# A decoder trunk on one core: x loaded tile by tile into another ring, its squares taken off GpSimd, small loads queued later

## The chip, the cores and the metric

The kernel runs on one core of one Trainium2 chip. The metric is the time of one execution in microseconds (us), lower is better. Three runs of the kernel before took 2304.75, 2304.87 and 2307.06 us, median 2304.87 us. The core has a matrix engine (TensorE, "PE" in the profile, with its weight loads "PEld"), a vector engine (VectorE, "DVE"), an activation engine (ScalarE, "ACT"), a general engine (GpSimd, "POOL") and a queue engine (SyncE, "SP") that only issues DMA transfers. ACT and POOL issue DMA transfers too, each on a queue of its own.

## The reference

One decoder layer in float32, 512 tokens of width 2048. Three sub-layers follow one another, each on a root-mean-square norm of x and added back to x: a mixer of three head groups (dilated window attention A, forgetting attention B, gated linear attention C), a cross-attention into 256 memory tokens, and a gated feed-forward network with a short causal convolution. A last norm closes it. The part that the change touches is the very first step:

```
def rms_norm(x, g):
    y = x * rsqrt(mean(x * x, axis=-1) + EPS)
    return y * g

proj = rms_norm(x, norm_mix) @ w_in     # 2048 -> 6168, split into the three groups' inputs
```

## The kernel before, in words

**Number format.** Each float32 operand of a large product is split in two parts of a faster format, `hi` (a rounded copy, made on ACT) and `lo` (the rest, made on DVE), and each product is three matmuls: hi by hi, hi by lo, lo by hi. So a weight tile needs one ACT and one DVE instruction for each half (L355, L356 in `weights`), and a tile of x needs one of each too (L322, L323 in `split_to`; they fold in the norm's gain, from a small table `gains`).

**x and its layout.** x is held transposed: 16 tiles, each 128 features by 512 tokens (256 KB). In memory two tiles lie side by side, in 512 KB blocks.

**The first stage.** `mixer` begins with `nat_units` on `w_first` (408 columns: the values of three head pairs of group A, the forget gates and the rank-16 gate). It has eight units. Unit u loads one block of weights (408 KB; L344) and works on the x tiles 2u and 2u+1. Four accumulators in PSUM, one for each 128 tokens, stay open over all 16 tiles; a tile of x meets each in three matmuls (L410 to L412). That is 192 matmuls of 408 columns. `xtile(k)` is called when a unit first needs tile k: it loads, splits and squares it. For k even, `raw_tile` loads the pair of tiles in one transfer (L1034); the first pair alone goes in two (L1032).

**The rings.** The pairs of x lie in the same ring of five 4 KB slots (`wraw`, WR = 5) as the raw weight blocks, in turn: weights, pair, weights, pair. A load waits until the last reader of its slot is done. The split weights have a ring of five half blocks (WS = 5). A ring of six tiles, `str`, in the pool `mc` (`stream`), is not used until later: it then holds parts of the mixer's output and the first six tiles of the residual.

**The sums of squares.** `square` adds the squares of the tiles up in two tiles `ls` (even k and odd k). Tiles 0 and 1 are squared on POOL directly (L1040); for the others ACT makes the square (L1044) and DVE adds it for odd k, POOL for even k (L1046). After tile 15, `stats` takes the sums over features with 16 narrow matmuls (L436), and DVE and POOL make the factor of each token from it, `rsx` (L439, L440). The accumulators are read out with that factor (`evac_v` at L629 and L630, then L890).

**Small loads.** The identity (64 KB), the causal mask `tri` (64 KB) and the convolution's coefficients `conv` (86 KB) are loaded on ACT's queue; the identity at L248, the others written after the first stage (L893, L894) but free to go earlier. The small operands of the gates and of the relative bias are loaded on POOL's queue (L642 to L726), 12 transfers, each ordered behind `self.begun`, which is POOL's addition for x tile 6.

**What sets the order.** The program is written in Python order; a planner then puts the instructions of each engine into a fixed order by modelled times and priorities, and each engine runs its list strictly in that order, waiting where data are missing. `issue_after` adds one fixed order between two instructions of an engine. Eight warm-up matmuls on a tile of ones come first on PE (L253).

After the first stage come the other input projections, with the gates, the relative bias and the gated linear attention worked in between, then attention A and B, the output projection, cross-attention and the feed-forward network, which holds half of the time.

Of the kernel before, what the change touches and what calls it, by code (L numbers as in the profile page):

```python
# [12 lines left out]
F32 = mybir.dt.float32  # L13
F32R = mybir.dt.float32r
I32 = mybir.dt.int32
AF = mybir.ActivationFunctionType
ALU = mybir.AluOpType
AX = mybir.AxisListType

P = 128  # L20
D = 2048
KT = D // P
S = 512
# [19 lines left out]
HT = S // 2  # L43
# [30 lines left out]
W_X = 8  # L74
WARM = 8
M0 = 8
H0 = 4
H1 = 6
ST = 4
# [148 lines left out]
class _Trunk:  # L228
    def __init__(self, tc, es, d, out):
        self.tc, self.es, self.nc, self.d, self.out = tc, es, tc.nc, d, out  # L230
        nc = tc.nc
        self.con = es.enter_context(tc.tile_pool(name="con", bufs=1))
        self.wp = es.enter_context(tc.tile_pool(name="wp", bufs=1))
        self.mc = es.enter_context(tc.tile_pool(name="mc", bufs=1))
        self.ps = es.enter_context(tc.tile_pool(name="ps", bufs=1, space=bass.MemoryType.PSUM))
        self.dr = es.enter_context(tc.tile_pool(name="dr", bufs=1, space=bass.MemoryType.DRAM))
        edge = es.enter_context(tc.tile_pool(name="edge", bufs=1, side="right"))
        edge.tile([P, 8], F32, name="edge")
        self.es_xp = ExitStack()
        self.xp = self.pool(self.es_xp, "xp", "right")  # L240
        self.bg = deque()
        self.credit = self.rate = 0
        nc.scalar.preload_act_table_set("natural_log_exp_and_others")
        con = self.con
        self.gains = con.tile([P, 5 * KT], F32, name="gains")
        nc.scalar.dma_start(out=self.gains, in_=d["gains"])
        self.ident = con.tile([P, P], F32, name="ident")
        nc.scalar.dma_start(out=self.ident, in_=d["c_ident"])  # L248
        self.ones = con.tile([P, P], F32, name="ones")
        nc.gpsimd.memset(self.ones, 1.0)  # L250
        warm = self.pst("W")
        for _ in range(WARM):
            nc.tensor.matmul(warm[:, :P], self.ones, self.ones, start=True, stop=True)  # L253
        self.eps = con.tile([P, 1], F32, name="eps")
        nc.gpsimd.memset(self.eps, EPS)
        self.onesr = con.tile([P, P], F32R, name="onesr")
        nc.scalar.activation(self.onesr, self.ones, AF.Copy)
        self.mhalf = con.tile([P, 16], F32, name="mhalf")
        nc.gpsimd.memset(self.mhalf, -0.5)
        self.conv = con.tile([P, 4 * FT], F32, name="conv")  # L260
        self.tri = con.tile([P, P], F32, name="tri")

    def pool(self, es, name, side):
        return es.enter_context(self.tc.tile_pool(name=name, bufs=1, side=side, reuse_waits="tile"))
# [594 lines left out]
    def mixer(self):  # L859
        nc, d, tc = self.nc, self.d, self.tc  # L860
# [15 lines left out]
        xs = {}  # L876
        parts = [self.pretile([P, S], i) for i in range(2)]

        def xtile(k):
            if k not in xs:  # L880
                raw = self.raw_tile(d["xT"], k, S, k == 0)
                xs[k] = self.split_gain(raw, self.gain(0, k))
                self.square(k, raw, parts, lambda n: self.pretile([P, n], 2 + k % 2))
                if k == KT - 1:
                    self.rs, self.spread = self.stats(parts, S, "x")
            return xs[k]

        def evac_first(t, ps):
            self.evac_v(t, ps, "a", 0, 3)
            self.turn = nc.scalar.activation(self.fg[:, t, :], ps[:, 384:G0], AF.Copy, scale=self.rs[:, t:t + 1])  # L890

        self.run(self.nat_units(d["w_first"], 0, xtile, NT, evac_first, True))
        nc.scalar.dma_start(out=self.tri, in_=d["c_tri"])  # L893
        nc.scalar.dma_start(out=self.conv, in_=d["conv"])  # L894
        xl = [xs[k] for k in range(KT)]

        def evac_c(dst, scale, j):
# [88 lines left out]
        for n in range(4, KT):  # L986
            for u in units[n]:
                u()
                if n >= M0:
                    next(mem, None)  # L990
# [32 lines left out]
        if sqs is not None:  # L1023
            self.square(dt, x1, sqs, tmp)

    def raw_tile(self, src, k, n, split=False):
        per = 1024 // n
        if k % per == 0:
            self.raw = self.wp.tile([P, per, n], F32, name="xraw", tag="wraw", bufs=WR, padded_shape=[P, 1024 // n, n])
            if split:  # L1030
                for i in range(per):
                    self.nc.sync.dma_start(out=self.raw[:, i, :], in_=src[k // per, :, i, :])  # L1032
            else:
                self.nc.sync.dma_start(out=self.raw, in_=src[k // per])  # L1034
        return self.raw[:, k % per, :]

    def square(self, dt, x, sqs, tmp):
        nc = self.nc
        if dt < 2:
            nc.gpsimd.tensor_tensor(sqs[dt], x, x, op=ALU.mult)  # L1040
        else:
            n = x.shape[-1]
            sq = tmp(n)
            nc.scalar.activation(sq, x, AF.Square)  # L1044
            eng = nc.vector if dt % 2 else nc.gpsimd
            added = eng.tensor_tensor(sqs[dt % 2], sqs[dt % 2], sq, op=ALU.add)  # L1046
            if eng is nc.gpsimd:
                self.pooled = added
                if dt == 6:
                    self.begun = added  # L1050

    def cross(self):
# [25 lines left out]
        def more(n):  # L1080
            for k in range(len(hs), min(len(hs) + n, KT)):
                hs.append(self.split_gain(self.x1[k], self.gain(1, k)))

        for i, u in enumerate(first):
            more((i >= H0) + (i >= H1))
            u()
# [426 lines left out]
    def ffn(self):  # L1513
# [55 lines left out]
        def chunk(c):  # L1569
# [9 lines left out]
            for k in range(n):  # L1579
                if c == 0 and k < len(self.early):  # L1580
                    load(c, k, self.early[k])
                else:
                    if not own:
                        self.last_gate()
                        open_fp()
                    parts = self.gated(p0 + k, stage[(k if c else k - len(self.early)) % len(stage)])
                    if c:
                        with tc.issue_after(self.mark.ins):
                            load(c, k, parts)
                    else:  # L1590
                        load(c, k, parts)
                plain = columns(raw_tile(d["w_d2"][p0 + k][:, :768], 768), (512, 256))
                sums = columns(raw_tile(self.two[p0 + k], 1024), (512, 512))
                for js, blocks in (((1, 2, 3), plain), (ADDED, sums)):
                    for i, j in enumerate(js):
                        for q in range(2):
                            mm(ps[j][:, q * HT:(q + 1) * HT], blocks[2 * i + q], k, j, k == 0 and q == 0,
                               k == n - 1 and q == 1)
# [39 lines left out]
            for q in range(6):  # L1638
# [6 lines left out]
                def made(i, *terms):  # L1645
                    if pre:
                        return raw_tile(pre[i], n * P)
                    tt(terms[0], terms[0], terms[1], ALU.add)
                    return terms[0]
# [159 lines left out]
```

## Time and profile before

| | us |
|---|---|
| median of three runs | 2304.87 |
| the profiled execution | 2308.35 |
| its span in the trace | 2306.2 |
| PE busy | 2282.7 |
| DVE busy | 1845.7 |
| ACT busy | 1242.3 |
| POOL busy | 204.9 |
| mean granted PE clock | 0.998 of full |

The span is the time from the trace's first to its last instruction. The profiled execution took 2.15 us more than its span. "Busy" of PE is modelled: matmuls overlap, and their ends are worked out, so what counts in the rows below is the distance between the starts of two matmuls.

### The profile page before, as it was taken

Reading aid. Unit: us, or ns where it says so; the run is one execution under the profiler, and the core shown is the slowest. Engines: PE = TensorE matmul, PEld = TensorE weight load, DVE = VectorE, ACT = ScalarE, POOL = GpSimd, SP = SyncE. Lnnn points to the kernel's source line nnn. Section 1 sums busy time; section 2 is a strip of 40 time slices with the busy share of each in tenths; the row PEclk is TensorE's granted clock in tenths of the full one; section 3 lists DMA queues with packets and bytes.
Section 4 is the critical chain, followed back from the end, with each engine's and each line's share of the span. In section 5 each row is a group of like instructions: output and inputs, shape, how many; then the busy total and the mean of one; then the engine's idle time right before and its main releaser. Section 6 shows DMA issues by size and latency. Waiting matters only on the chain.

```text
span 2306.2 us, 42646 instructions
## 1 busy us (share of the span) xinstructions
PE 2282.7 (99%) x15948; PEld 2140.1 (93%) x15948; DVE 1845.7 (80%) x3620; ACT 1242.3 (54%) x2545; POOL 204.9 (9%) x278
## 2 busy tenths in 40 slices
PE   9999999999999999999999999999999999999997
PEld 8798898888778888899999999999999999999997
DVE  7825666666797355699999999999999898999887
ACT  6323345655575254585555555555555575747454
POOL 3000000000002011121111111100000020101003
PEclk9999999999999999999999999999999999999999
DMA  6432122223224358587777778753334493736432
GB/s 217 152 97 83 49 98 91 93 87 96 87 80 153 110 180 218 132 233 180 214 209 213 205 209 215 199 184 122 130 126 140 142 337 103 277 115 230 154 122 84
DMA packets 130836, 355.47 MB, mean 154 GB/s; under 512 B 13653, under 2 KB 45333, under 8 KB 130181
## 3 DMA queue, kind: packets, MB, share of 16 engines
q1 hardware_dynamic: 87264, 268.28, 34.5%
q0 software_dynamic: 37168, 73.91, 14.6%
q10 hardware_dynamic: 6196, 10.57, 1.4%
q8 instruction: 125, 2.05, 0.4%
q14 instruction: 83, 0.67, 0.1%
HBM read 325.65 MB, written 76.07 MB: 174 GB/s over the span
## 4 chain that ended last, share of the span: by engine, by line
PE 91%; DVE 4%; DMA 2%; ACT 2%; issue 1%; POOL 0%; DVEq 0%; SPq 0%; ACTq 0%
PE acc L369 18%; PE acc L371 18%; PE acc L370 18%; PE psC L371 5%; PE psC L369 5%; PE psC L370 5%; PE psD L370 3%; PE psD L369 3%; PE psD L371 3%; PE acc L410 2%; PE acc L411 2%; PE acc L412 2%; PE psS L783 1%; PE psT L551 1%; PE psQ L371 1%; PE psQ L370 1%
## 5 line engine op out<-in xcount | busy, mean ns | idle before, releaser
L330 ACT ACTIVATE whi<-wraw 128x512 fp32r<-128x512 f32 (+2 forms) x814 | 466.1, 602 | 431.7 <-DVE wraw L1384 177.2
L331 DVE TENSOR_TENSOR wlo<-wraw,whi 128x512 fp32r<-128x512 f32 (+2 forms) x814 | 517.1, 655 | 83.5 <-ACT whi L330 78.8
L371 PE MATMUL acc<-sum,wlo 128*128 128x256 f32 x1956 | 549.3, 281 | 0.9 <-DVE wlo L331 0.8
L370 PE MATMUL acc<-sum,whi 128*128 128x256 f32 x1956 | 549.7, 281 | 0.0
L369 PE MATMUL acc<-sum,whi 128*128 128x256 f32 x1956 | 548.4, 280 | 0.0
L356 DVE TENSOR_TENSOR wlo<-wraw,whi 128x512 fp32r<-128x512 f32 (+2 forms) x336 | 223.0, 671 | 200.3 <-ACT whi L355 199.2
L355 ACT ACTIVATE whi<-wraw 128x512 fp32r<-128x512 f32 (+2 forms) x336 | 203.3, 610 | 325.1 <-PE acc L370 210.1
L371 PEld LDWEIGHTS acc<-sum,wlo 128*128 128x128 f32 x1956 | 368.5, 188 | 1.7 <-DVE wlo L331 1.7
L369 PEld LDWEIGHTS acc<-sum,whi 128*128 128x128 f32 x1956 | 368.5, 188 | 0.6 <-ACT whi L330 0.4
L370 PEld LDWEIGHTS acc<-sum,whi 128*128 128x128 f32 x1956 | 367.9, 188 | 0.0
L369 PE MATMUL acc<-xhi,whi 128*128 128x512 f32 (+1 forms) x848 | 334.8, 395 | 0.4 <-ACT fg L890 0.4
L371 PE MATMUL acc<-xhi,wlo 128*128 128x512 f32 (+1 forms) x848 | 329.1, 388 | 0.0
L370 PE MATMUL acc<-xlo,whi 128*128 128x512 f32 (+1 forms) x848 | 328.5, 388 | 0.0
L371 PE MATMUL psC<-sum,wlo 128*128 128x256 f32 x928 | 261.1, 281 | 0.0
L369 PE MATMUL psC<-sum,whi 128*128 128x256 f32 x928 | 260.3, 280 | 0.0
L370 PE MATMUL psC<-sum,whi 128*128 128x256 f32 x928 | 259.7, 280 | 0.0
L371 PEld LDWEIGHTS acc<-xhi,wlo 128*128 128x128 f32 x848 | 159.4, 188 | 32.0
L369 PEld LDWEIGHTS acc<-xhi,whi 128*128 128x128 f32 x848 | 159.6, 188 | 29.1 <-ACT fg L890 0.8
L370 PEld LDWEIGHTS acc<-xlo,whi 128*128 128x128 f32 x848 | 159.8, 188 | 28.5 <-DVE xlo L318 0.2
L369 PEld LDWEIGHTS psC<-sum,whi 128*128 128x128 f32 x928 | 175.0, 189 | 0.0
L370 PEld LDWEIGHTS psC<-sum,whi 128*128 128x128 f32 x928 | 174.7, 188 | 0.0
L371 PEld LDWEIGHTS psC<-sum,wlo 128*128 128x128 f32 x928 | 174.5, 188 | 0.0
(401 smaller groups left out, 4359.3 us busy)
## 6 DMA issues: line engine op xcount, KB each, us to landing
wraw<-in_w_up SPq DMA_DIRECT2D x127, 512.0 KB, 6.2
b<-in_w_up SPq DMA_DIRECT2D x42, 512.0 KB, 4.5
wraw<-in_w_o SPq DMA_DIRECT2D x32, 512.0 KB, 3.5
wraw<-in_w_d SPq DMA_DIRECT2D x34, 448.0 KB, 4.4
wraw<-in_w_d SPq DMA_DIRECT2D x36, 384.0 KB, 4.6
wraw<-in_w_qka SPq DMA_DIRECT2D x24, 512.0 KB, 3.5
gd<-sq SPq DMA_DIRECT2D x40, 256.0 KB, 6.2
wraw<-two SPq DMA_DIRECT2D x20, 512.0 KB, 5.5
```

The costliest lines, as they stand in the source:

```text
L330: nc.scalar.activation(hi, r, AF.Copy)
L331: nc.vector.tensor_tensor(lo, r, hi.bitcast(F32), op=ALU.subtract)
L355: nc.scalar.activation(hi, r, AF.Copy)
L356: nc.vector.tensor_tensor(lo, r, hi.bitcast(F32), op=ALU.subtract)
L369: nc.tensor.matmul(out, lh, rh, start=start, stop=False, skip_group_check=more)
L370: nc.tensor.matmul(out, lh, rl, start=False, stop=False, skip_group_check=more)
L371: last = nc.tensor.matmul(out, ll, rh, start=False, stop=stop, skip_group_check=more)
L410: self.nc.tensor.matmul(o, xh[:, tt], wh, start=(k == 0), stop=False)
L411: self.nc.tensor.matmul(o, xh[:, tt], wl, start=False, stop=False)
L412: self.last = self.nc.tensor.matmul(o, xl[:, tt], wh, start=False, stop=(k == KT - 1))
L551: nc.tensor.transpose(tp[:, b * P:(b + 1) * P], pt[:, b * P:(b + 1) * P], self.ident)
L783: nc.tensor.matmul(sc[:, c * 64:(c + 1) * 64], kk[:, c * P:(c + 1) * P], qe[:, c * 64:(c + 1) * 64], start=True, stop=True)
```

## The change

Each x tile is loaded by itself, into the six-tile ring `str`; tile 0 in two halves of 256 tokens, which are split one after the other. The squares of tiles 0 and 1 are made by ACT, and all 14 additions by DVE. `self.begun` becomes a copy of one column of x tile 8 (the ninth) on POOL, and the loads of the identity, `tri` and `conv` go to POOL's queue directly behind it, ahead of the 12 loads that were there. `raw_tile` keeps its second use, in the residual after the output projection.

```
-        nc.scalar.dma_start(out=self.ident, in_=d["c_ident"])
...
-                raw = self.raw_tile(d["xT"], k, S, k == 0)
-                xs[k] = self.split_gain(raw, self.gain(0, k))
-                self.square(k, raw, parts, lambda n: self.pretile([P, n], 2 + k % 2))
+                raw = self.stream(0)
+                xs[k] = hi, lo = self.xslot()
+                cuts = [slice(0, HT), slice(HT, S)] if k == 0 else [slice(0, S)]
+                for c in cuts:
+                    nc.sync.dma_start(out=raw[:, c], in_=d["xT"][k // 2, :, k % 2, c])
+                for c in cuts:
+                    self.split_to(hi[:, c], lo[:, c], raw[:, c], self.gain(0, k))
+                if k < 2:
+                    nc.scalar.activation(parts[k], raw, AF.Square)
+                else:
+                    sq = self.pretile([P, S], 2 + k % 2)
+                    nc.scalar.activation(sq, raw, AF.Square)
+                    nc.vector.tensor_tensor(parts[k % 2], parts[k % 2], sq, op=ALU.add)
+                if k == M1:
+                    self.begun = nc.gpsimd.tensor_copy(self.mark1, raw[:, :1])
+                    with tc.issue_after(self.begun.ins):
+                        for t, src in ((self.ident, "c_ident"), (self.tri, "c_tri"), (self.conv, "conv")):
+                            nc.gpsimd.dma_start(out=t, in_=d[src])
...
-        nc.scalar.dma_start(out=self.tri, in_=d["c_tri"])
-        nc.scalar.dma_start(out=self.conv, in_=d["conv"])
```

## Rows read from the trace of the kernel before

**Rows 1.** The page: busy time, share of the span and instructions of each engine; and the chain that ended last, as shares of the span by engine.

```profile
PE 2282.7 (99%) x15948; PEld 2140.1 (93%) x15948; DVE 1845.7 (80%) x3620; ACT 1242.3 (54%) x2545; POOL 204.9 (9%) x278
...
PE 91%; DVE 4%; DMA 2%; ACT 2%; issue 1%; POOL 0%; DVEq 0%; SPq 0%; ACTq 0%
```

**Rows 2.** Windows: for each stretch its length, then the busy time (and count of instructions) of PE, PEld, DVE, ACT and POOL, the granted PE clock, the mean busy share of the DMA engines, and GB/s moved.

```profile
5.00:10.00 5.00, 3.60 (x14) 3.21 (x15) 3.33 (x5) 2.48 (x5) 1.75 (x2) 0.82 0.93 327
...
48.47:100.00 51.53, 50.70 (x229) 40.11 (x230) 44.74 (x80) 21.30 (x42) 1.27 (x5) 1.00 0.33 116
```

**Rows 3.** Timeline of PE, the first 12 us: start, duration, engine, line, operation, tiles, count, and in brackets the idle time before it and what ended that.

```profile
1.00 3.79 PE L253 MATMUL psW<-ones 128*128 128x128 f32 x16 [1.00 <-POOL ones L250]
5.40 0.45 PE L410 MATMUL acc<-whi,xhi 128*128 128x408 f32 x1 [0.62 <-ACT xhi L322]
...
6.42 0.34 PE L412 MATMUL acc<-whi,xlo 128*128 128x408 f32 x1
...
7.76 0.45 PE L410 MATMUL acc<-whi,xhi 128*128 128x408 f32 x1 [1.00 <-ACT whi L355]
...
8.29 0.54 PE L410 MATMUL acc<-whi,xhi 128*128 128x408 f32 x1
...
11.35 0.46 PE L412 MATMUL acc<-whi,xlo 128*128 128x408 f32 x1
```

**Rows 4.** Timeline of PE, from 26 us to the first matmul of the next stage (L369).

```profile
26.81 0.35 PE L411 MATMUL acc<-wlo,xhi 128*128 128x408 f32 x1
27.52 0.45 PE L412 MATMUL acc<-whi,xlo 128*128 128x408 f32 x1 [0.36 <-DVE xlo L323]
...
35.95 0.35 PE L412 MATMUL acc<-whi,xlo 128*128 128x408 f32 x1
...
37.83 0.45 PE L411 MATMUL acc<-wlo,xhi 128*128 128x408 f32 x1 [0.95 <-DVE wlo L356]
...
38.31 0.35 PE L410 MATMUL acc<-whi,xhi 128*128 128x408 f32 x1
...
42.19 1.84 PE L436 MATMUL psT<-ones,ls 128*128 128x1 f32 x16
43.89 0.44 PE L410 MATMUL acc<-whi,xhi 128*128 128x408 f32 x1
...
47.69 0.35 PE L412 MATMUL acc<-whi,xlo 128*128 128x408 f32 x1
48.47 0.50 PE L369 MATMUL acc<-xhi,whi 128*128 128x512 f32 x1 [0.44 <-ACT fg L890]
```

**Rows 5.** Timeline of ACT, the first four splits.

```profile
3.50 0.54 ACT L355 ACTIVATE whi<-wraw 128x408 fp32r<-128x408 f32 x1 [1.16 <-DMA wraw<-in_w_first]
...
4.63 0.72 ACT L322 ACTIVATE xhi<-xraw,gains 128x512 fp32r<-128x512 f32 x1 [0.58 <-DMA xraw<-in_xT]
6.56 0.72 ACT L322 ACTIVATE xhi<-xraw,gains 128x512 fp32r<-128x512 f32 x1 [1.21 <-DMA xraw<-in_xT]
7.19 0.53 ACT L355 ACTIVATE whi<-wraw 128x408 fp32r<-128x408 f32 x1
```

**Rows 6.** DMA issues in the first 60 us: tiles, queue, count, KB each, median us from issue to landing.

```profile
xraw<-in_xT SPq DMA_DIRECT2D x7, 512.0 KB, 5.0
wraw<-in_w_first SPq DMA_DIRECT2D x7, 408.0 KB, 4.1
xraw<-in_xT SPq DMA_DIRECT2D x2, 256.0 KB, 3.4
...
conv<-in_conv ACTq DMA_DIRECT2D x1, 86.0 KB, 4.6
```

**Rows 7.** Groups of DVE's instructions from 0 to 48.5 us, each shape apart: line, tiles, count, then busy us and mean ns of one, and idle time before them.

```profile
L323 DVE SCALAR_TENSOR_TENSOR xlo<-xraw,gains,xhi 128x512 fp32r<-128x512 f32 x16 | 16.9, 1068 | 4.6 <-ACT xhi L322 4.6
L356 DVE TENSOR_TENSOR wlo<-wraw,whi 128x408 fp32r<-128x408 f32 x16 | 11.2, 719 | 4.3 <-ACT whi L355 4.3
L1046 DVE TENSOR_TENSOR ls<-ls,ls 128x512 f32<-128x512 f32 x7 | 4.8, 679 | 0.0
```

**Rows 8.** Timelines of POOL and of DVE: a POOL addition and the DVE instruction beside it; then the last of POOL's small loads and the DVE instructions beside it.

```profile
22.26 1.31 POOL L1046 TENSOR_TENSOR ls<-ls,ls 128x512 f32<-128x512 f32 x1
...
21.91 2.11 DVE L356 TENSOR_TENSOR wlo<-wraw,whi 128x408 fp32r<-128x408 f32 x1
...
28.34 0.51 POOL L726 DMA_DIRECT2D ln<-in_c_lnm x1
...
28.49 1.40 DVE L323 SCALAR_TENSOR_TENSOR xlo<-xraw,gains,xhi 128x512 fp32r<-128x512 f32 x2
```

**Rows 9.** Timelines of SP and of ACT: the issue of the last pair of x, and the first reader of it.

```profile
29.95 0.33 SPq L1034 DMA_DIRECT2D xraw<-in_xT x1
...
34.69 0.72 ACT L322 ACTIVATE xhi<-xraw,gains 128x512 fp32r<-128x512 f32 x1 [1.64 <-DMA xraw<-in_xT]
```

**Rows 10.** Groups of ACT's instructions from 0 to 48.5 us, columns as in rows 7.

```profile
L322 ACT ACTIVATE xhi<-xraw,gains 128x512 fp32r<-128x512 f32 x16 | 11.4, 714 | 5.7 <-DMA xraw<-in_xT 5.6
L1044 ACT ACTIVATE ls<-xraw 128x512 f32<-128x512 f32 x14 | 8.6, 617 | 2.8 <-DVE ls L1046 2.8
L355 ACT ACTIVATE whi<-wraw 128x408 fp32r<-128x408 f32 x16 | 8.2, 532 | 2.3 <-DMA wraw<-in_w_first 1.6 <-PE acc L412 0.6
```

**Rows 11.** Timelines of DVE and ACT: the first reader of the identity, and the first reader of the gates' small weights.

```profile
45.78 0.29 DVE L446 TENSOR_SCALAR diag<-ident,rsx 128x128 f32<-128x128 f32 x1 [0.94 <-POOL rsx L440]
...
53.21 0.52 ACT L656 ACTIVATE w<-w 112x384 fp32r<-112x384 f32 x1
```

More of the change, by code (lines that the diff above doesn't have):

```diff
@@ L76 @@
 M0 = 8
+M1 = 8
 H0 = 4
@@ L261, in __init__ @@
         self.tri = con.tile([P, P], F32, name="tri")
+        self.mark1 = con.tile([P, 1], F32, name="mark1")
     def pool(self, es, name, side):
@@ L1024, in resid, with raw_tile @@
             self.square(dt, x1, sqs, tmp)
-    def raw_tile(self, src, k, n, split=False):
+    def raw_tile(self, src, k, n):
         per = 1024 // n
@@ L1029, in raw_tile @@
             self.raw = self.wp.tile([P, per, n], F32, name="xraw", tag="wraw", bufs=WR, padded_shape=[P, 1024 // n, n])
[L1030 to L1034, printed above, removed]
+            self.nc.sync.dma_start(out=self.raw, in_=src[k // per])
         return self.raw[:, k % per, :]
@@ L1048, in square @@
                 self.pooled = added
-                if dt == 6:
-                    self.begun = added
     def cross(self):
```

## The prediction

> **What bounds the kernel now.** I read the page's first and fourth parts first: PE is busy 99% of the span and makes up 91% of the chain that ended last [rows 1]. So an edit pays only where it removes time in which PE waits or runs slowly, and every edit here lies in the first stage, up to the first matmul of line L369 at 48.47 us. I then read PE's timeline there by the distance between the starts of matmuls. At full clock a 408-column matmul follows the last by 0.185 us: from 38.31 to 42.19 there are 21 steps, 3.88 / 21 [rows 4]. The stage has 192 such matmuls, 35.5 us, and the statistics' narrow ones take 1.7 us (42.19 to 43.89). That makes 37.2 us; from the first matmul at 5.40 [rows 3] to 48.47 it took 43.07. So 5.8 us were lost, in three places:
>
> - *The start, 2.9 us.* Between 6.42 and 7.76 PE has no second x tile and no second half of the first weights: 1.34 minus one step, 1.15. From 8.29 to 11.35 nine matmuls are 0.34 apart, where a full step is 0.185, and the granted clock from 5 to 10 us is 0.82 [rows 2, 3], a mixture of full speed (2.4 GHz) and half (1.2 GHz); before that fall PE had two holes. The slow steps cost 9 x 0.155 = 1.4. Longer steps at each restart add 0.3.
> - *The middle, 2.3 us.* 26.81 to 27.52 behind an `xlo` of DVE (0.5), 35.95 to 37.83 mostly behind a `wlo` of DVE (two steps of 0.185 have become 1.88: 1.5 lost), restarts 0.3 [rows 4].
> - *The end, 0.6 us.* 47.69 to 48.47 behind the read-out of the first accumulator [rows 4].
>
> Besides, the warm-up ends at 4.79 (1.00 + 3.79) and the first real matmul starts at 5.40 [rows 3]: 0.6 us to be had ahead of the stage. All together 6.4 us. After the stage PE is busy 50.70 of 51.53 us [rows 2], so a stage that ends earlier hands its gain on, if the planner's order behind it stays much as it is.
>
> **The change part by part.**
>
> *Tile 0 in halves.* The first matmul waits for `xhi` of the whole tile, started when its 256 KB are there, at 4.63, after `whi` ended at about 4.04 [rows 5]. With halves 128 KB have to land, and a half split takes about half of 0.71, so `xhi` for the first tokens is ready near 4.5 and PE can go on from the warm-up at 4.79. Bounds: 0 and 0.6; I take 0.5.
>
> *The order of the first transfers, and the identity, `tri` and `conv` off ACT's queue.* Before, SP issued first half of weights, tile 0, tile 1, second half; ACT then split tile 1 at 6.56 and only behind it the second half at 7.19, and PE went on at 7.76 [rows 3, 5]. Now tile 1 comes behind the second half. It has 204 KB more ahead of it on SP's queue, but 214 KB (64 + 64 + 86) have left the first microseconds; `conv` alone was on its way for 4.6 us [rows 6]. At 327 GB/s [rows 2] 204 KB are 0.6 us. If all of the 214 KB would have moved before tile 1, the two cancel and tile 1 lands near 6.5; if none, near 7.2. Its split takes 0.7, and the weights are ready by then. PE has 12 matmuls on tile 0, 12 x 0.185 = 2.2 us from 4.79, to 7.0. So PE waits between 0.2 and 0.9. With the lower value the hole is gone, and so, I think, is the stretch at half clock behind it; with the upper one both stay. Bounds 0 and 2.9; I take 2.2, nearer to the first, because the 214 KB share the same microseconds.
>
> *Rings.* Weights and x no longer share five slots: five blocks of weights and six tiles of x (three units) can be under way, where it was two and a half units of both. The last pair of x was issued at 29.95, when a slot came free, and its split started at 34.69, which ACT spent 1.64 us waiting for [rows 9]. That lateness is what stands behind the `wlo` at 37.83, since ACT and DVE do the tiles and the weights in a fixed order. With loads three units ahead it goes.
>
> *Squares off POOL.* DVE gets seven more additions, 7 x 0.68 = 4.8 us [rows 7]. But POOL's additions held DVE up: the `wlo` at 21.91, 0.57 us elsewhere, took 2.11, until after the addition that POOL ran from 22.26 to 23.57 [rows 8]. Beside POOL's DMA issues nothing of the kind is seen: two `xlo` from 28.49 took 1.40 together, with an issue at 28.34 [rows 8]. The mean `xlo` is 1.07 and `wlo` 0.72 [rows 7]; undisturbed about 0.70 (1.40 / 2) and 0.57. So DVE's work for the stage becomes 16 x 0.70 + 16 x 0.57 + 14 x 0.68 = 29.8 us, against 32.9 before (16.9 + 11.2 + 4.8), in a stage of 37.2. If the disturbed means stayed it would be 37.6, just over PE's own time: this is the other bound. ACT gets two squares: 16 x (0.71 + 0.62 + 0.53) = 29.8 us [rows 10]; also under 37.2. Of the 2.3 us in the middle I take 2.1, bounds 0 and 2.3. Cover is thin rather than ample: per unit PE needs 4.4 us, ACT and DVE 3.7 each.
>
> *The end.* The statistics still stand at the same place in the program, behind the first tokens' part of tile 14, so the chain statistics, POOL's power, read-out is as long as before. I take 0, bounds 0 and 0.6.
>
> *Small loads and the new wait.* POOL's copy waits for tile 8, and behind it are queued 15 DMA issues of some 0.51 us [rows 8], 7.7 us, and POOL's power for `rsx`. Tile 8 has to be there before PE's fifth unit, at the latest at 4.79 + 4 x 4.4 = 22.5. The issues then end by 30.2, and a landing of 4.6 us more [rows 6] makes 35, if the last loads go as `conv` did. Readers: the identity at 45.78, the gates' weights at 53.21 [rows 11]; both come some 5 us earlier now, at 41 and 48. Cost 0; if tile 8 came after 29 us, each further microsecond would be a late one for the identity or for the gates.
>
> Sum: 0.5 + 2.2 + 2.1 = 4.8 us. The profiled execution took 2308.35 us (span 2306.2 and 2.15 around it), 3.5 above the median of 2304.87; its first stage has no reason to be longer than in the others, so I take the gain off the median: 2300.1, say 2300.0 us.
>
> The Trainium skill, "DMA: Bandwidth & Descriptors" (Bandwidth, Measured), has a rule that speaks against one tile at a time: batch transfers to at least 1 MiB, since each carries a fixed cost near 2 us. By the formula of its section Anatomy of one DMA (made for POOL's queue), 2.0 us and bytes by 436 GB/s, an estimate, a pair is 3.2 us as one transfer and 5.2 as two, and seven pairs would cost 14 us if nothing overlapped. This case's rows have 5.0 us for 512 KB and 3.4 for 256 KB, so a fixed part is there (third rival).
>
> **The rivals.** A change under 0.2% (4.6 us) can't be told from none here.
>
> 1. *The start stays as it is.* Tile 1 lands at 7.2, PE has its hole and its half clock; only the middle and half of the first 0.6 are gained: 2.4 us, 2302.5. For it: x tile 1 is now last of five transfers. Against it: 214 KB less beside them. 12%.
> 2. *DVE becomes the bound.* The two kinds of split stay at their disturbed means; 37.6 us of work after a first `wlo` at about 4 us leave PE waiting as before: gain 0.8, 2304.0. For it: DVE gets seven more additions, and is at 80% over the whole kernel [rows 1]. Against it: what disturbed it was POOL's arithmetic, which goes. 9%.
> 3. *The loads become the bound: slower.* Place: SP's queue, seven pairs of x. Two transfers of 256 KB in series take 6.8 us against 5.0 for one of 512 KB [rows 6], 1.8 more for each pair, 12.6 for seven. With none of the gain the time is 2304.9 + 12.6 = 2317.5; if half of it is hidden, 2311. It decides from the point at which a unit's three transfers take over 4.4 us, so if few are in flight together. Against it: 327 GB/s were reached with several in flight [rows 2], and a unit's 920 KB need 2.8 us at that rate. 11%, with whatever else of that sign the new order behind the stage brings.
> 4. *All goes, the end too:* 6.4 us, 2298.5 or a little below. 8%.
>
> **How the numbers follow.** The forecast, 60%, has a gain of 3.2 to 6.0 around 4.8, so 2299 to 2301.7; since 4.6 lies inside, I put 42 of the 60 above it and 18 below. Faster: 42 + 8 = 50%. Within 0.2%: 18 + 12 + 9 = 39%. Slower: 11%. The range goes from just below the fourth rival, 2297, to the second, 2304.8; what is left out is the third and a little below.
>
> **What would show it.** In the changed profile the first L410 stands at about 4.8 to 5.0; the hole after 12 matmuls is under 0.3 us and no stretch of 0.34 us steps follows; no `xlo` or `wlo` of the stage is over 1 us, and POOL has no arithmetic beside them but one short copy; SP issues x three units ahead; the first L369 starts near 43.5 instead of 48.47, and the stages behind it keep their lengths. The prediction is wrong if L369 comes early and the time does not move (given back later), if the half clock is still there, or if ACT's splits wait for x.

## The result, and the profile after

The changed kernel takes 2314.88 us (median of 6 runs, 2314.36 to 2317.78) against 2305.26 for the kernel before, timed beside it. The ratio is 1.0045, interval 1.0034 to 1.0056: 9.6 us slower, where 4.8 us faster was forecast. The profiled execution took 2314.94 us, span 2313.2. Lines in helpers are numbered one higher than before: L411 to L413 are the products of the first stage, L370 to L372 those of the next, L324 and L357 the low halves of x and of the weights.

**The first stage did become shorter.** The page's engines and its chain by engine, to be laid beside [rows 1]:

```profile
PE 2292.5 (99%) x15948; PEld 2139.9 (93%) x15948; DVE 1844.3 (80%) x3628; ACT 1244.8 (54%) x2548; POOL 195.3 (8%) x273
...
PE 95%; DVE 2%; ACT 1%; issue 0%; POOL 0%; DMA 0%; SPq 0%; DVEq 0%; ACTq 0%
```

DVE, DMA and ACT have left the chain to PE (95% instead of 91%), and yet PE's own busy time is 9.8 us longer, with the same 15948 matmuls. PE's timeline over the first stage, answering to [rows 3, 4]:

```profile
1.00 3.78 PE L253 MATMUL psW<-ones 128*128 128x128 f32 x16 [1.00 <-POOL ones L250]
6.60 0.45 PE L411 MATMUL acc<-whi,xhi 128*128 128x408 f32 x1 [1.81 <-ACT xhi L323]
6.89 0.35 PE L412 MATMUL acc<-wlo,xhi 128*128 128x408 f32 x1
...
44.19 0.35 PE L413 MATMUL acc<-whi,xlo 128*128 128x408 f32 x1
44.90 0.50 PE L370 MATMUL acc<-xhi,whi 128*128 128x512 f32 x1 [0.36 <-ACT fg L906]
```

PE starts 1.20 us later than before (6.60 for 5.40), then runs without an idle time that the timeline shows until the last product, and reaches the next stage at 44.90 instead of 48.47: 3.57 us early. DVE's groups up to 45 us show why the middle no longer waits, beside [rows 7]:

```profile
L324 DVE SCALAR_TENSOR_TENSOR xlo<-str,gains,xhi 128x512 fp32r<-128x512 f32 x15 | 11.2, 746 | 0.0
L894 DVE TENSOR_TENSOR ls<-ls,ls 128x512 f32<-128x512 f32 x14 | 9.6, 683 | 0.0
L357 DVE TENSOR_TENSOR wlo<-wraw,whi 128x408 fp32r<-128x408 f32 x16 | 9.0, 578 | 4.9 <-ACT whi L356 4.9
```

An `xlo` takes 746 ns instead of 1068, a `wlo` 578 instead of 719; with seven more additions DVE has 30.7 us of work here (0.9 of it for tile 0's halves) where it had 32.9.

**Then the gain is lost, a little at every matmul.** Windows of the changed kernel; the first two answer to [rows 2]:

```profile
5.00:10.00 5.00, 3.40 (x18) 3.33 (x19) 3.19 (x6) 4.48 (x10) 0.00 (x0) 1.00 0.98 351
...
48.47:100.00 51.53, 50.80 (x225) 39.59 (x225) 44.57 (x75) 18.74 (x34) 2.07 (x7) 1.00 0.38 131
100.00:200.00 100.00, 100.00 (x541) 94.44 (x540) 39.57 (x83) 32.14 (x59) 2.89 (x3) 1.00 0.36 116
200.00:300.00 100.00, 100.00 (x573) 88.55 (x573) 65.99 (x217) 37.31 (x92) 8.46 (x9) 1.00 0.17 53
...
700.00:800.00 100.00, 100.00 (x442) 80.43 (x442) 52.46 (x93) 41.66 (x84) 16.42 (x16) 1.00 0.42 137
```

The same stretches after the first stage in the kernel before:

```profile
100.00:200.00 100.00, 100.00 (x546) 94.62 (x545) 41.47 (x86) 32.00 (x59) 3.66 (x4) 1.00 0.38 125
200.00:300.00 100.00, 100.00 (x579) 89.23 (x579) 66.58 (x218) 37.96 (x93) 8.43 (x9) 1.00 0.17 55
...
700.00:800.00 100.00, 100.00 (x452) 82.59 (x452) 51.56 (x85) 41.24 (x83) 17.42 (x17) 1.00 0.42 142
```

PE is busy for the whole of each stretch in both, at the full granted clock in both, and gets through 1% to 2% fewer matmuls: 541 for 546, 573 for 579, 442 for 452. So it is neither a wait nor the clock; single matmuls take longer. Laying the two kernels' matmuls side by side by their number in the order of execution, the changed kernel is 2.33 us ahead at the 500th (108.5 us), 0.71 ahead at the 1000th, 0.89 behind at the 2000th, 3.53 behind at the 3000th, 9.24 behind at the 4800th (960 us), and from there on 7 to 9 behind to the end.

The groups of the 512-column products of x, the kernel before first:

```profile
L369 PE MATMUL acc<-xhi,whi 128*128 128x512 f32 x816 | 325.8, 399 | 0.4 <-ACT fg L890 0.4
L371 PE MATMUL acc<-xhi,wlo 128*128 128x512 f32 x816 | 319.9, 392 | 0.0
L370 PE MATMUL acc<-xlo,whi 128*128 128x512 f32 x816 | 319.4, 392 | 0.0
```

and the changed one:

```profile
L370 PE MATMUL acc<-xhi,whi 128*128 128x512 f32 x816 | 328.8, 403 | 0.4 <-ACT fg L906 0.4
L371 PE MATMUL acc<-xlo,whi 128*128 128x512 f32 x816 | 323.5, 397 | 0.0
L372 PE MATMUL acc<-xhi,wlo 128*128 128x512 f32 x816 | 323.4, 397 | 0.0
```

These durations overlap; what counts is the step from one start to the next. Its median over these 2448 matmuls rose from 227 ns to 233 or 234, and the steps' sum from 574.6 us to 585.3, +10.7. The 384- and 512-column products with the weights as the moving operand add 2.5. (Of a product's two operands one is loaded by PEld and stays, the stationary one; the other streams past it, the moving one, and gives the columns.) With the start 1.2 us later, the first stage's own steps 4.8 shorter, and nothing for the products of the cross-attention's output (their step stays 227), that is 9.7; other groups are 0.5 shorter together, and 9.15 us is what the 5000th matmul shows. These steps account for the loss.

**What differs is an address.** The change allocates one tile that no part of its description speaks of: `mark1`, 4 bytes a partition for POOL's copy, which the pool rounds to 32 bytes. It stands ahead of everything on the left side of SBUF, so in the built program the halves of the weights lie 32 bytes higher (`whi` at 35296 for 35264, `wlo` at 45536 for 45504), while x's halves, on the right side, stay (`xhi` at 163776). The cross-attention's output also lies on the left, and moved together with the weights.

### The profile page after: what moved, and what is told of

The parts are those of the page before. It is cut to its first block, busy times and chain, and to the rows that moved or that the text cites. A ratio compares the mean times of both kernels' runs of the same rounds, so it can differ in the third digit from the quotient of the medians.

```text
span 2313.2 us, 42661 instructions
## 1 busy us (share of the span) xinstructions
PE 2292.5 (99%) x15948; PEld 2139.9 (93%) x15948; DVE 1844.3 (80%) x3628; ACT 1244.8 (54%) x2548; POOL 195.3 (8%) x273
## 4 chain that ended last, share of the span: by engine, by line
PE 95%; DVE 2%; ACT 1%; issue 0%; POOL 0%; DMA 0%; SPq 0%; DVEq 0%; ACTq 0%
PE acc L370 19%; PE acc L372 19%; PE acc L371 19%; PE psC L370 5%; PE psC L372 5%; PE psC L371 5%; PE acc L411 3%; PE acc L412 3%; PE acc L413 3%; PE psD L370 3%; PE psD L372 3%; PE psD L371 3%; PE psS L784 1%; PE psT L552 1%; PE psQ L370 1%; PE psQ L372 1%
## 5 line engine op out<-in xcount | busy, mean ns | idle before, releaser
L370 PE MATMUL acc<-sum,whi 128*128 128x256 f32 x1956 | 550.1, 281 | 0.0
L372 PE MATMUL acc<-sum,wlo 128*128 128x256 f32 x1956 | 548.8, 281 | 0.0
L357 DVE TENSOR_TENSOR wlo<-wraw,whi 128x512 fp32r<-128x512 f32 (+2 forms) x336 | 221.4, 665 | 209.8 <-ACT whi L356 206.8
L370 PEld LDWEIGHTS acc<-sum,whi 128*128 128x128 f32 x1956 | 368.8, 189 | 0.2
L372 PEld LDWEIGHTS acc<-sum,wlo 128*128 128x128 f32 x1956 | 368.5, 188 | 0.0
L370 PE MATMUL acc<-xhi,whi 128*128 128x512 f32 (+1 forms) x848 | 337.8, 399 | 0.4 <-ACT fg L906 0.4
L372 PE MATMUL acc<-xhi,wlo 128*128 128x512 f32 (+1 forms) x848 | 332.6, 392 | 0.0
L370 PE MATMUL psC<-sum,whi 128*128 128x256 f32 x928 | 260.7, 281 | 0.0
L372 PE MATMUL psC<-sum,wlo 128*128 128x256 f32 x928 | 260.4, 281 | 0.0
L372 PEld LDWEIGHTS acc<-xhi,wlo 128*128 128x128 f32 x848 | 159.4, 188 | 35.2
L370 PEld LDWEIGHTS acc<-xhi,whi 128*128 128x128 f32 x848 | 159.5, 188 | 32.6 <-ACT fg L906 0.7
L372 PEld LDWEIGHTS psC<-sum,wlo 128*128 128x128 f32 x928 | 174.9, 188 | 0.1
L370 PEld LDWEIGHTS psC<-sum,whi 128*128 128x128 f32 x928 | 174.7, 188 | 0.0
```

The lines of the kernel that those rows point to most:

```text
L357: nc.vector.tensor_tensor(lo, r, hi.bitcast(F32), op=ALU.subtract)
L370: nc.tensor.matmul(out, lh, rh, start=start, stop=False, skip_group_check=more)
L372: last = nc.tensor.matmul(out, ll, rh, start=False, stop=stop, skip_group_check=more)
```

## The experiments

Two theories stood at first. By one, the weights' place in SBUF relative to x's sets the step. By the other, the new order of instructions does it, whatever the addresses. All experiments but the second start from the changed kernel.

**1. 64 bytes instead of 32.** The order of instructions is that of the changed kernel, instruction for instruction.

```
-self.mark1 = con.tile([P, 1], F32, name="mark1")
+self.mark1 = con.tile([P, 16], F32, name="mark1")
```

> The changed kernel, with its new one-column tile 64 bytes wide instead of 32, so that everything allocated behind it (the weight rings among it) lies 64 and not 32 bytes further than in the kernel before; every engine's list of instructions is the same as in the changed kernel. Theory A (a product is slower where the weights' tiles and x's tiles lie 32 bytes apart modulo 64): the 512-column steps fall back from 233 to 228 ns, 12.5 us go, and what stays is the first stage's gain of 3.6 us: 2305.3 - 3.6 = 2301.7 us. Theory B (the loss is in the new order behind the first stage, or in the loads): 2314.9 us, as the changed kernel.

Measured: 2312.49 (2310.84 to 2315.23), ratio 1.0032, interval 1.0021 to 1.0043. A miss for 512 columns, which stay at 233 ns; but the 384-column steps went back from 175 to 173. So the place matters, and a multiple of 64 is not what the 512-column step needs.

**2. The kernel before, with an unused tile of 32 bytes.** No instruction differs.

```
+con.tile([P, 1], F32, name="gap")
```

> The kernel before, with nothing changed but an unused tile of 32 bytes at the place where the changed kernel has its one-column tile. Theory A: 512-column steps of 233 ns on x and 176 to 177 ns for the 384-column ones: 2305.3 + 12.5 = 2317.8 us. Theory B: 2305.3 us.

Measured: 2318.1 (2317.58 to 2320.18), ratio 1.0056, interval 1.0043 to 1.0069. A hit: an empty tile alone makes the kernel before some 13 us slower, with a median step of 234 ns. The address alone is enough for the loss; no new order of instructions is needed.

**3. x moved as well.** `mark1` stays at its 32 bytes, and a filler at the other end of SBUF is 32 bytes wider, so that x's tiles move too.

```
-edge.tile([P, 8], F32, name="edge")
+edge.tile([P, 16], F32, name="edge")
```

> The changed kernel with the filler tile at the other end of the memory 64 bytes wide instead of 32, so that x's tiles move by 32 bytes as well, towards the other end, and both have the same place modulo 64 again, though not the place of before. Same instruction lists as the changed kernel. If it is the distance between the two operands modulo 64 that counts: 2301.7 us, as with the 64-byte tile. If it is the weights' own place modulo 64 (or x's): 2314.9 us or more.

Measured: 2313.32 (2311.91 to 2313.99), ratio 1.0032, interval 1.002 to 1.0045. Neither of the two times that were expected. The addresses of all operands are different from experiment 1, their distance modulo 256 is the same (192), and so are the steps: 233 ns for 512 columns and 173 for 384. The weights stand where they stand in the changed kernel, whose 384-column steps are 175, so it is not their own place that decides. It goes by the distance.

**4. The squares of tiles 0 and 1 behind the split of tile 1** (with the 64 bytes of experiment 1).

```
+raws.append(raw)
+if k == 1:
+    with tc.issue_after(self.cut.ins):
+        for j in range(2):
+            nc.scalar.activation(parts[j], raws[j], AF.Square)
```

> The changed kernel with the 64-byte tile, and the squares of x tiles 0 and 1 ordered on ACT behind the split of tile 1. Against the run with the 64-byte tile alone: the first matmul on x waits no more for the square of tile 0 (0.53 us) nor for the second half of that tile, so it starts at 4.9 to 5.5 instead of 6.6 us and the time falls by 0.5 to 1.7 us, if the first stage stays bound by PE; if ACT's list is the limit there, it does not move.

Measured: 2311.33 (2311.1 to 2314.28), ratio 1.0028, interval 1.0017 to 1.0039. PE starts at 4.46 instead of 6.13, then waits 0.99 us for tile 1 at 7.73, and reaches the next stage at 44.23, as in experiment 1 (44.24). The median is 1.2 us below experiment 1, inside what was expected, but the runs of the two overlap (2310.84 to 2315.23 there), and the profiles show no gain: an earlier start on tile 0 alone brings nothing, since tile 1's arrival takes it back.

**5. No new tile at all**: the mark goes into the unused rest of another small tile. Every address is as before, every instruction as in the changed kernel.

```
-self.eps = con.tile([P, 1], F32, name="eps")
+eps = con.tile([P, 2], F32, name="eps")
+self.eps, self.mark1 = eps[:, :1], eps[:, 1:]
```

> The changed kernel with the one-column tile moved into the unused rest of the tile that holds EPS, so that every tile has the address that it had in the kernel before; the engines' lists are those of the changed kernel. If addresses alone explain the loss behind the first stage, the 512-column steps on x are 228 ns as before and the time is the first stage's gain below the kernel before: 2304.9 - 3.6 to 4.2 = 2300.7 to 2301.3 us. If the new order costs something besides, more: up to 2312.

Measured: 2303.13 (2301.3 to 2305.42, 11 runs), before 2304.74 (27 runs), ratio 0.9991, interval 0.9982 to 1.0. The 512-column steps are 227 ns again: 11.75 us of the changed kernel's 2314.88 were the address (11.2 if each is taken against the kernel before timed beside it). The time is still 1.8 to 2.4 us above what was expected: the first stage gives less than the 3.57 us that the profile of the changed kernel showed (experiment 7). The groups of this kernel, beside the two above:

```profile
L370 PE MATMUL acc<-xhi,whi 128*128 128x512 f32 x816 | 325.6, 399 | 0.5 <-ACT fg L906 0.5
L372 PE MATMUL acc<-xhi,wlo 128*128 128x512 f32 x816 | 319.7, 392 | 0.0
L371 PE MATMUL acc<-xlo,whi 128*128 128x512 f32 x816 | 319.3, 391 | 0.0
```

**6. The period: `mark1` of 128, 256 and 512 bytes.**

```
-self.mark1 = con.tile([P, 1], F32, name="mark1")
+self.mark1 = con.tile([P, 64], F32, name="mark1")
```

(32 and 128 columns for the other two.)

> The changed kernel with the one-column tile 128 bytes wide. The distance from the weights' tiles to x's, modulo 512, which was 0 before (1536 bytes modulo 2048), becomes 384. The runs with distances of 480 (32 bytes) and 448 (64 bytes, and the other end moved) both had 233 ns. If the distance must be a multiple of 128: 228 ns and 2301 us. If it must be a multiple of 256 or 512: 233 ns and 2312 us.

> The same with 256 bytes: distance 256 modulo 512. Multiple of 128 or 256 enough: 228 ns and 2301 us; multiple of 512 needed: 233 ns and 2312 us.

> The same with 512 bytes: distance 0 modulo 512, but 1024 instead of 1536 modulo 2048. If the distance modulo 512 (or a divisor of it) decides: 228 ns and 2301 us. If it is not the distance between these two but the place of something else, or the distance modulo 2048: 233 ns and 2312 us.

Measured: 2314.98 (ratio 1.0046, interval 1.0033 to 1.006), 2303.35 (0.9993, 0.9984 to 1.0002) and 2303.11 (0.9992, 0.9983 to 1.0001). The period is 256 bytes. Over all runs so far, the median step by the distance of the moving from the stationary operand, modulo 256 bytes:

| distance | 512 columns | 384 columns | kernels |
|---|---|---|---|
| 0 | 227 ns | 173 ns | before, experiment 5, `mark1` of 256 and 512 bytes |
| 32, 224 | 234 ns | 175 ns | the changed kernel, experiment 2 |
| 64, 192 | 230 to 233 ns | 173 ns | experiments 1, 3, 4 |
| 128 | 232 ns | 175 ns | `mark1` of 128 bytes |

**7. Which edit gives the first stage's gain?** Three kernels each undo one part of experiment 5. Squares and their additions as before, half of these on POOL:

```
-if k < 2:
-    nc.scalar.activation(parts[k], raw, AF.Square)
-else:
...
-    nc.vector.tensor_tensor(parts[k % 2], parts[k % 2], sq, op=ALU.add)
+self.square(k, raw, parts, lambda n: self.pretile([P, n], 2 + k % 2))
```

> As no_gap, but the squares of x's tiles are added as in the kernel before, half of them on GpSimd. With everything else of the change kept and the weights' addresses as before, this asks whether GpSimd's additions are what held the middle of the first stage (2.1 us in the sum). If so the 512-column steps begin near 47.5 to 48 us instead of 45.2 to 46.4 and the kernel takes about 2305; if they were beside the work all along, 45.2 to 46.4 and 2303. Steps stay 227 ns in both.

x in pairs through the weights' ring, as before:

```
-raw = self.stream(0)
-xs[k] = hi, lo = self.xslot()
...
+raw = self.raw_tile(d["xT"], k, S, k == 0)
+xs[k] = self.split_gain(raw, self.gain(0, k))
```

> As no_gap, but x comes in pairs through the weights' ring as before, and the rest of the change stays. If the loading by single tiles is what gives the gain of the first stage, the hole at 5.8 us or another one comes back, the 512-column steps begin near 47.5 to 48.5 us and the time is about 2305; if the additions or the small loads give it, they begin at 45.2 to 46.4 and the time stays at 2303.

The three small loads on ACT's queue, as before:

```
+nc.scalar.dma_start(out=self.ident, in_=d["c_ident"])
...
-for t, src in ((self.ident, "c_ident"), (self.tri, "c_tri"), (self.conv, "conv")):
-    nc.gpsimd.dma_start(out=t, in_=d[src])
...
+nc.scalar.dma_start(out=self.tri, in_=d["c_tri"])
+nc.scalar.dma_start(out=self.conv, in_=d["conv"])
```

> As no_gap, but the three small loads are issued on ScalarE's queue as before, one ahead of all squares. Priced at 0 in the prediction: the 512-column steps begin at 45.2 to 46.4 us and the time is 2303 plus or minus 1. If instead ScalarE's issues delay the first splits, about half a microsecond to 1 us later.

Measured, beside 2304.82 for the kernel before: 2305.34 (ratio 1.0002, interval 0.9992 to 1.0011), 2302.75 (0.999, 0.9981 to 1.0) and 2303.52 (0.9993, 0.9983 to 1.0002). With POOL's additions the time came out as if these held the middle, in the other two as if their part made no difference. Against the kernel before they differ by little more than their intervals, but the ten runs of the first (2304.66 to 2306.66) all lie above the ten of the second (2301.83 to 2304.61); the profiles show where. From the first product of x to the first L370 or its like:

| kernel | first product | next stage | between |
|---|---|---|---|
| before | 5.40 | 48.47 | 43.07 |
| experiment 2 (before and 32 bytes) | 5.86 | 49.60 | 43.74 |
| squares with POOL | 4.54 | 47.40 | 42.86 |
| changed | 6.60 | 44.90 | 38.30 |
| experiment 5 | 6.79 | 46.38 | 39.59 |
| `mark1` of 256, 512 bytes | 6.22, 6.47 | 46.08, 45.20 | 39.86, 38.73 |
| x in pairs | 6.06 | 45.51 | 39.45 |
| small loads on ACT | 6.12 | 45.75 | 39.63 |

The three kernels with POOL's additions need 42.9 to 43.7 us, the others 38.3 to 39.9. Of the three parts only the squares change the time; rings (with tile 0 whole again) and small loads make no difference that shows in it.

Two things blur the table, which has one profile for each kernel. With POOL's squares the first product comes earlier, and some of the 42.86 us is waiting at the start, up to 8.79 us, as in experiment 4. And in some profiles PE makes nine or ten steps of 0.34 us between 6.7 and 11.5 us, where a full one is 0.19, worth some 1.4 us: with them (experiments 3, 5 and 8, `mark1` of 128 and 256 bytes) the next stage starts at 45.83 to 46.52, without them (the changed kernel, experiment 1, `mark1` of 512 bytes) at 44.24 to 45.20. The kernel with POOL's additions has no such stretch and still comes at 47.40.

DVE's groups up to 45 us in the kernel with POOL's additions:

```profile
L324 DVE SCALAR_TENSOR_TENSOR xlo<-str,gains,xhi 128x512 fp32r<-128x512 f32 x15 | 14.0, 958 | 0.0
L357 DVE TENSOR_TENSOR wlo<-wraw,whi 128x408 fp32r<-128x408 f32 x16 | 13.2, 850 | 4.1 <-ACT whi L356 4.1
L1051 DVE TENSOR_TENSOR ls<-ls,ls 128x512 f32<-128x512 f32 x7 | 7.0, 997 | 0.0
```

and in experiment 5:

```profile
L324 DVE SCALAR_TENSOR_TENSOR xlo<-str,gains,xhi 128x512 fp32r<-128x512 f32 x15 | 11.2, 746 | 0.1
L894 DVE TENSOR_TENSOR ls<-ls,ls 128x512 f32<-128x512 f32 x14 | 9.6, 683 | 0.0
L357 DVE TENSOR_TENSOR wlo<-wraw,whi 128x408 fp32r<-128x408 f32 x16 | 9.1, 579 | 5.7 <-ACT whi L356 5.7
```

With POOL beside it DVE's `wlo` takes 850 ns instead of 579, its `xlo` 958 instead of 746, and even with seven additions fewer it has more to do (34.2 us for 29.9). PE then waits for it, in the one gap that the timeline of that kernel shows between 22 us and the next stage:

```profile
31.96 0.46 PE L412 MATMUL acc<-wlo,xhi 128*128 128x408 f32 x1 [1.46 <-DVE wlo L357]
47.40 0.50 PE L370 MATMUL acc<-xhi,whi 128*128 128x512 f32 x1 [0.46 <-ACT fg L901]
```

The Trainium skill ("SBUF — State Buffer", Who interferes with whom) says that a VectorE instruction with two inputs in SBUF contends with a GpSimd instruction that reads SBUF; the 850 ns against 579 agree. The same section says that PE waits on nobody for its reads of SBUF, with independent ports for its two operands. Taken as a rule for the time of a product this does not hold here: with steps of 227 ns in the kernel before and 234 in experiment 2, which differ in no instruction, the places of the two operands do bear on each other. Whether it is their reads that collide is not shown.

**8. The feed-forward's tiles of sums at one distance.** In the kernel before they alternate in place by 8 columns, and the distance of a sum's tile from the weights cycles through 32, 96, 160 and 224 bytes. In the runs above a 256-column step had its lowest median, 113 to 116 ns by operand, at 192, and 116 to 120 elsewhere. From experiment 5:

```
-SHIFT = 8
+SHIFT = 0
...
 put(sx, order)
+sx.tile([P, 16], F32, name="pad")
...
-put(self.pool(self.es_fa, "fa", "left"), own)
+fa = self.pool(self.es_fa, "fa", "left")
+fa.tile([P, 48], F32, name="pad")
+put(fa, own)
```

> As no_gap, but all tiles of token sums stand at one distance from the weights' halves, 192 bytes modulo 256, where they cycle through several distances in the kernel before. Outputs are the same. If the distance of the operands sets the step there too, the some 10,600 256-column products of the feed-forward fall from 117.5 ns to 115 ns a step, worth 25 to 27 us: 2276 to 2280. If these products are bound by something else, 2303; if the alternation of the sums' places protected something, above 2303.

Measured: 2295.19 (2294.35 to 2296.84), ratio 0.9957, interval 0.9942 to 0.9972. This is faster than both kernels, by 9.6 us against the one before and by 19.7 against the changed one, but 7.9 us below experiment 5 is a third of what was expected of the distance. Windows of this kernel show where it came from:

```profile
1400.00:1600.00 200.00, 200.00 (x1701) 200.00 (x1700) 187.03 (x296) 107.45 (x191) 16.51 (x21) 1.00 0.63 182
...
2060.00:2100.00 40.00, 40.00 (x355) 40.00 (x354) 35.40 (x66) 22.04 (x49) 0.54 (x1) 1.00 0.40 126
2100.00:2150.00 50.00, 50.00 (x443) 50.00 (x442) 46.52 (x102) 37.07 (x91) 6.98 (x13) 1.00 0.77 270
```

and two of experiment 5:

```profile
1400.00:1600.00 200.00, 200.00 (x1698) 200.00 (x1697) 186.72 (x293) 108.22 (x193) 13.20 (x17) 1.00 0.60 177
...
2100.00:2150.00 50.00, 50.00 (x426) 50.00 (x425) 44.85 (x103) 37.49 (x95) 7.52 (x14) 1.00 0.83 284
```

From 1400 to 1600 us it does 1701 matmuls for 1698, no gain; from 2100 to 2150 it does 443 for 426, a step of 113 ns for 117. Taken in stretches of 25 us its steps have a median of 118 or of 113 to 114, and nearly nothing between: 118 for most of 1025 to 2000, 113 from 2050 on. With one distance throughout PE has two rates. The trace shows where they change: only where the stream is broken. Of twelve changes ten follow a single step of 159 to 1057 ns, and two follow a few products of the tile `cell`, which stands at distance 0; in between a rate holds, once over 6328 products. One such place, with five steps of 114 ns on average before a wait and four of 117 behind it:

```profile
1089.65 0.28 PE L371 MATMUL acc<-sum,whi 128*128 128x256 f32 x1
...
1090.22 0.28 PE L370 MATMUL acc<-sum,whi 128*128 128x256 f32 x1
1090.33 0.28 PE L371 MATMUL acc<-sum,whi 128*128 128x256 f32 x1
1091.13 0.39 PE L372 MATMUL acc<-sum,wlo 128*128 128x256 f32 x1 [0.52 <-DVE wlo L332]
1091.35 0.28 PE L370 MATMUL acc<-sum,whi 128*128 128x256 f32 x1
...
1091.82 0.28 PE L371 MATMUL acc<-sum,whi 128*128 128x256 f32 x1
```

Not every long step changes the rate, and why one does was not found.

## Why the prediction was wrong

The step that failed is "the stages behind it keep their lengths", with "hands its gain on" before it. The sum had no term for the 32-byte tile of the new copy. It was counted as "one short copy" of POOL's time, and its place was counted at nothing. That missing term is +11.75 us (experiment 5 against the changed kernel), and it has the only say in the sign. No rival held it either: the slower one had its place in SP's queue, and x in pairs against x in single tiles (2302.75 and 2303.13) shows no loss there at all. That 2314.88 lies between the two times worked out for that rival (2311 and 2317.5) is chance. Its rider, a loss by the new order behind the stage, is ruled out by experiment 5, which has that order and no loss. The prediction did name this course among what would show it wrong: the next stage early, and the gain given back later.

Without the address the change gives 2303.13, a gain of 1.6 us with an interval of 0 to 4.1 (0.9982 of 2304.74), where 4.8 was summed. By its terms:

- *Tile 0 in halves, 0.5.* Wrong in sign for the first product, which came at 6.60 instead of 4.8. ACT's timeline of the changed kernel, beside [rows 5], shows two reasons:

```profile
5.52 0.63 ACT L890 ACTIVATE ls<-str 128x512 f32<-128x512 f32 x1 [1.35 <-DMA str<-in_xT]
6.05 0.90 ACT L323 ACTIVATE xhi<-str,gains 128x256 fp32r<-128x256 f32 x2
```

  The square of the tile stands ahead of its two half splits, so it waits for both halves and then takes its 0.53 us first; and the tile lands at 5.5 instead of 4.6. In the first 5 us 139 GB/s were moved, 186 before; why is not settled. In the three kernels that load tile 0 whole it landed at 4.63 to 5.09, in those that load it in halves the second half at 5.04 to 5.96, so the halves themselves may cost some of it. Experiment 4 takes the square out of the way and PE starts at 4.46, but the term still comes to nothing, since tile 1 then stops it.
- *The start's hole and half clock, 2.2.* In the changed kernel both are gone (granted clock 1.00 from 5 to 10 us, 0.82 before). But the later first product costs 1.2 of it, and in experiment 5 the clock was at 0.79 in those microseconds, with nine steps of 0.34 us, while its first product came 1.4 later. So of the 2.9 us some 1.7 came back in the changed kernel and next to nothing in experiment 5. Kernels with the same instructions differ in it: `mark1` of 512 bytes has no such step, and 256 bytes has ten from 6.73 us on, though the clock column reads 1.00 there (the trace's first entry for the clock is at 10.25 us).
- *The middle, 2.1.* Right in size and in mechanism as far as DVE goes: the `xlo` and `wlo` lost their disturbed durations (746 and 578 ns, forecast 700 and 570). The part given to the rings was not needed: x in pairs has 39.45 us and the same time.
- *The end, 0.* Right: 44.19 to 44.90, where it was 47.69 to 48.47.
- *Small loads, 0.* Right. POOL's issues stood between the copy and the power for `rsx` with room to spare, and with three of them back on ACT's queue the time is 2303.52:

```profile
16.38 0.82 POOL L896 COPY mark<-str 128x1 f32<-128x1 f32 x1 [14.59 <-DMA str<-in_xT]
...
25.26 0.51 POOL L727 DMA_DIRECT2D ln<-in_c_lnm x1
40.74 1.43 POOL L441 TENSOR_TENSOR rsx<-rsx,mhalf 128x4 f32<-128x4 f32 x1 [14.96 <-DVE rsx L440]
```

- *The third rival, and the rule of the Trainium skill beside it* ("DMA: Bandwidth & Descriptors", Bandwidth, Measured). It did not come about: loads of 256 KB moved 351 GB/s from 5 to 10 us with several in flight.

The gain of the first stage in the profiles (2.1 to 3.3 us at distance 0) is kept to the end: experiment 5 is 2.09 ahead at the next stage and 2.30 at the last matmul. So "hands its gain on" holds where the addresses stay.

## What to carry to other kernels

A new tile, however small, moves what is allocated behind it, and a stream of matmuls feels where its two operands lie relative to each other; so compare the addresses of the large operands before and after any edit that allocates, and put a small tile into an unused rest or pad it so that they don't move. When every stage becomes a little longer with PE busy and the clock full, look at the step from start to start per shape: waits and busy shares don't show it. An engine's own additions can be dearer on a free engine than on the busy one, if the free one slows the busy one down.

## What the runs showed of the hardware

At a granted clock of 1.00 the step of a 512-column product in this kernel is 227 ns if the SBUF addresses of the stationary and the moving operand differ by a multiple of 256 bytes, and 230 to 234 ns at the other distances tried (32, 64, 128, 192, 224); 384 columns take 173 ns at 0 and 64 and 175 at 32 and 128; the 408 columns of the first stage 186 or 187 at 0, 32 and 64, and 183 at 128 (one run). For 256 columns 0 is not the best: 118 to 120 ns at 0 and 113 to 116 at 192, and 113 or 118 in experiment 8, where all sums are at 192. Why 256 bytes, and why the narrow products differ from the wide ones, stays open; no run here looks into it.
